# A two-layer hybrid trunk on one core: other buffer counts in the state-space scan, and fewer score maxima ahead of the latent attention

## The chip, the cores and the metric

The kernel runs on one core of one Trainium2 chip. The metric is device time in microseconds from the start to the end of one execution. Besides plain runs there is one execution taken by the hardware profiler. From it come the profile page and the trace that is queried in the text. A core has five engines, each working through its own instructions in order: TensorE (PE; its weight loads are listed as PEld), VectorE (DVE), ScalarE (ACT), GpSimd (POOL) and SyncE (SP). SP does no arithmetic here; it issues almost all DMA transfers. "SPq" and the like name an engine's queue.

## The reference, cut to what matters

Two layers run over 1024 latent tokens and 128 context tokens of width 1024, all in float32. Layer 0 has a window attention and a bidirectional state-space scan beside each other, with one output projection. Layer 1 is a multi-head latent attention with 16 heads. The parts that the change touches:

```python
# layer 0, scan, per chunk of 128 tokens and per head (16 heads, two directions)
decay = jnp.exp(jnp.where(causal, cum_l - cum_s, -inf))
scores = einsum(c, b) * decay
y = scores @ (x * dt) + (c @ h_in) * exp(cum)          # within the chunk + from the state
y = y_f + flip(y_b) + d_skip * xs
s_out = rms_norm(y * silu(z), gnorm_w)                 # gated norm
out = concat([a_out, s_out]) @ w_out                   # projection, then the residual add
...
# layer 1, per head
p = softmax(q @ k.T * scale)                           # latent tokens read 1024 + 128 keys
o = p @ v
```

The softmax needs one number per query that is near the row's maximum, so that the exponentials stay in range. Since the same number is taken off the numerator and the denominator, it need not be the maximum itself.

## The kernel before

**Order of the work.** The kernel is written as Python generators that issue instructions. The tile framework then orders each engine's instructions by a modelled timeline (line 1712), so the order on an engine is not that of the code. Only what goes through `keep_in_program_order` (`pinned`, `in_order`) stays where it was written. Memory is split into four arenas R, S, G and F; `Space.tile` gives a tile `bufs` buffers that take turns. A write to a buffer waits until its last reader is done. There is no other renaming: with `bufs=2` the tile after next shares the buffer.

**The scan, `scan_out` (lines 975 to 1037).** It runs once for each token tile c of 128 tokens: first the context tile (`NLT` = 8), then 0 to 7. It works with features on partitions and tokens along the row. Tiles 8 and 0 are issued beside the gates of layer 0 (`first_outputs`, line 1043). The others are issued in the loop at line 1158, each ahead of the projection (`project_out`) of the tile before.

A tile loads x in both layouts (`xs`, `y`), the gate path z (`zs`), the entering state (`H`) and the small factors B and C. `y`, `xs`, `zs` and `H` are 512 KB each. Then come four units u of four heads each. A unit does this:

- SP loads `cu` (line 1003, 512 KB): the cumulated decays of four heads and two directions, the same row to all 128 partitions.
- ACT takes exponentials for the state part (line 1008, two instructions), and DVE multiplies them by C into `Cx` (1009).
- POOL masks `cu` by direction (1012, two), ACT takes eight biased exponentials (1014), DVE adds the directions (1016) and multiplies by the scores `G` (1017). The result lies in `cu` itself.
- PE multiplies it, and `Cx`, into the accumulator `acc` (line 971, called from 1021).

After units 1 and 3 DVE adds the accumulator to half of `y` (1025) and multiplies that half by `zs` (1026). At the tile's end `split` (ACT copy, line 249; DVE subtraction, line 250) turns `y` into the two halves `sT` of the three-product matmul. ACT then squares `y` into the same `zs` buffer (1029), and DVE sums the squares (1031). `zs` is therefore held until line 1031 is done.

**The projection, `project_out` (line 1091).** It has 72 matmuls of 512 columns per tile, in two accumulators: `acca` for the attention part and `accs` for the scan part, which reads `sT`. Then come `L1105` to `L1108`, the norm of the next layer and its transposes (`L1062` to `L1067`).

**The latent attention's prelude (lines 1586 to 1612).** Heads go in pairs. A pair needs its operands (`AK`, `BK`, `AQ`, `BQ`), the values, and for each head a row of negated maxima in row 96 of `AQ`. `head_max` makes that row: for each token tile, three matmuls of 384 keys (line 1447) and a DVE maximum over each (recorded at line 209, where the step list calls it). The context tile has one of 128 keys. So a head has 8 x 3 + 1 = 25 of them (`NMAX`). After each group of token tiles come the negation (1426, 1427), a transpose on PE (1432), a copy (1437) and one row store per tile (1439). The groups are the tiles 0 to 3, the tiles 4 to 7 and the context tile. Ahead of pair 0 the code issues the values and all 50 maxima of heads 0 and 1.

**The main loop (lines 1614 to 1643).** `pair_main` yields 38 steps per pair: 18 for the queries 0 to 511, 18 for 512 to 1023, two for the context. A step makes one tile of scores (1468 to 1470), the exponential (1475) and, later, the product with the values (1489). `spread` lays other streams beside the steps, at most three units per step: the next pair's operands and the maxima of its two heads, from step 11 on.

Of the kernel before, what the change touches and what calls it, by code (L numbers as in the profile page):

```python
# [12 lines left out]
F32 = mybir.dt.float32  # L13
F32R = mybir.dt.float32r
# [11 lines left out]
NLT = NL // 128  # L26
KT = D // 128
# [193 lines left out]
def hybrid_trunk(ctx: ExitStack, tc: tile.TileContext, I, O, dbg=None, stage=99):  # L221
# [683 lines left out]
    p4, p = Space(mem), Space(mem)  # L905
# [69 lines left out]
    def scan_out(p, sp, c):  # L975
# [13 lines left out]
        y = p.tile([128, KT, 128], F32, tag="y", name="y", bufs=2)  # L989
        dma.dma_start(y, xT_d[:, :, tok].rearrange("k p n -> p k n"))  # L990
        pool.tensor_tensor(y, y, dskip.unsqueeze(2).broadcast_to([128, KT, 128]), ALU.mult)
        zs = p.tile([128, KT, 128], F32, tag="zs", name="zs", bufs=2)
        dma.dma_start(zs, z_d[:, :, tok].rearrange("k p n -> p k n"))
        if c < NLT:
            H = p.tile([128, D], F32, tag="Hc", name="Hc", bufs=2)
            dma.dma_start(H[0:64], H_d[c, 0:64])
            dma.dma_start(H[64:128], H_d[NLT - 1 - c, 64:128])
        for u in range(4):
            g, h0 = u // 2, c * 16 + u * 4
            if u % 2 == 0:  # L1000
                acc = psum("o" if c < NLT else "pre", "yacc")
            cu = p.tile([128, 4, 2, 128], F32, tag="cu", name="cu", bufs=2)
            dma.dma_start(cu, bcast_rows(cum_d[h0:h0 + 4], 128))
            if c < NLT:
                Cx = p.tile([128, 4, 128], F32, tag="Cx", name="Cx", bufs=2)
                for d in range(2):
                    r = slice(d * 64, (d + 1) * 64)
                    act.activation(Cx[r], cu[r, :, d], AF.Exp)  # L1008
                dve.tensor_tensor(Cx, Cx, BC[:, 1, g].unsqueeze(1).broadcast_to([128, 4, 128]), ALU.mult)
            for d in range(2):  # L1010
                s = 1 - 2 * d
                pool.affine_select(cu[:, :, d], cu[:, :, d], [[0, 4], [s, 128]], ALU.is_ge, NEG, base=0, channel_multiplier=-s)  # L1012
                for j in range(4):
                    act.activation(cu[:, j, d], cu[:, j, d], AF.Exp, bias=nb[:, d, h0 + j:h0 + j + 1])  # L1014
            m = cu[:, :, 0]
            dve.tensor_tensor(m, m, cu[:, :, 1], ALU.add)
            dve.tensor_tensor(m, m, G[:, g].unsqueeze(1).broadcast_to([128, 4, 128]), ALU.mult)
            todo = [(xs, m, j) for j in range(4)] + ([(H, Cx, j) for j in range(4)] if c < NLT else [])
            for n, (left, right, j) in enumerate(todo):
                a, b = j % 2, u % 2 * 2 + j // 2  # L1020
                in_order(n, acc[a * 64:(a + 1) * 64, b * 128:(b + 1) * 128], left[:, (u * 4 + j) * 64:(u * 4 + j + 1) * 64], right[:, j],
                         start=(u % 2 == 0 and n < 2), stop=(u % 2 == 1 and n >= len(todo) - 2))
            if u % 2:
                yg, ks = y[:, g * 4:g * 4 + 4], slice(g * 4, g * 4 + 4)
                dve.tensor_tensor(yg, acc.rearrange("p (k n) -> p k n", k=4), yg, ALU.add)
                dve.tensor_tensor(yg, yg, zs[:, ks], ALU.mult)
        sT = sp.tile([128, 2, KT, 128], F32R, tag="sT", name="sT", bufs=2)
        split(sT[:, 0], sT[:, 1], y)
        act.activation(zs, y, AF.Square)
        sq = p.tile([128, 128], F32, tag="sq", name="sq", bufs=1, at="G")  # L1030
        dve.tensor_reduce(sq, zs.rearrange("p k n -> p n k"), AX.X, ALU.add)
# [123 lines left out]
    with p5 as p:  # L1155
        gate = load_gate(p, 0, 1)
        prev = None
        for c in [NLT] + list(range(NLT)) + [None]:
            if c is not None:
                sT = sTs[c] if c in sTs else scan_out(p, op5, c)  # L1160
# [127 lines left out]
    steps = Steps()  # L1288
# [127 lines left out]
            after(1, place, Q, pr, uq_proj(qh, ql, pr * 128, cols), AQ, BQ, cols)  # L1416
            yield

    def head_max(h):

        s = h % NSET

# [15 lines left out]
            for t in range(n):  # L1438
                dma.dma_start(AQ[s][96:97, (t0 + t) * 128:(t0 + t + 1) * 128].bitcast(F32), mrow[t:t + 1].bitcast(F32))

        for t0, n in ((0, 4), (4, 4), (NLT, 1)):
            pm = p7.tile([128, 4, 3], F32, tag="pm", name="pm", bufs=3)
            spans = [(NL + 128, 128)] if t0 == NLT else [(c * CH, CH) for c in range(3)]
            for t in range(t0, t0 + n):
                for c, (k0, w) in enumerate(spans):
                    pp = spare("pp")
                    pe.matmul(pp[:, 0:w], AQ[s][0:96, t * 128:(t + 1) * 128], AK[s][0:96, k0:k0 + w], start=True, stop=True)  # L1447
                    after(1, dve.tensor_reduce, pm[:, t - t0, c:c + 1], pp[:, 0:w], AX.X, ALU.max)
                    if t == t0 + n - 1 and c == len(spans) - 1:
                        after(1, negate, t0, n, pm[:, 0:n, 0:len(spans)])  # L1450
                    yield
# [134 lines left out]
    NMAX = 25  # L1586
# [19 lines left out]
    mem.set("G", F32)  # L1606
    while len(AK) < NSET:
        operand_set()
    rows1 = head_max(1)
    for stream in (first, quad_values(0), head_max(0), rows1):  # L1610
        for _ in stream:
            steps.tick()
    p8, p9 = Space(mem, right=True), Space(mem)
    for pair in range(8):
        op = p7.tile([128, T], F32, tag="op", name="op")
        if pair < 7:
            Q = pair // 2 + 1
            make, n_make = [operands(pair + 1)], 22
            if pair % 2 == 0 and Q < 4:
                make += [quad_weights(Q), quad_rope(Q)]  # L1620
            aux = [(chain(*make), n_make, 0), (chain(head_max(2 * pair + 2), head_max(2 * pair + 3)), 2 * NMAX, 11)]
            if pair % 2:
                aux[0] = (aux[0][0], 22, 0)
                aux.append((quad_values(Q), NKT, 20))
            aux = spread(36, *aux)
            for _ in pair_main(pair, op):
# [89 lines left out]
```

## Time and profile before

| | us |
|---|---|
| median of 3 runs | 1871.18 |
| lowest and highest run | 1867.86 and 1876.07 |
| profiled execution | 1872.8 |
| its span, first to last instruction | 1871.0 |

| engine | busy us | share of the span |
|---|---|---|
| PE | 1696.0 | 91% |
| DVE | 1043.1 | 56% |
| ACT | 865.4 | 46% |
| POOL | 728.0 | 39% |

The shares are averages over stages with different limits. The mean granted clock of PE is 0.946. In the timeline the stages lie about so: modulation and first layer's projections to 350 us, convolutions and window attention to 640, gates and scan and output projection to 1000, the latent projections and gates to 1165, the attention to 1750, the final projection to the end.

### The profile page before, as it was taken

The numbers are of one execution on the slowest core, as the hardware profiler recorded it, in microseconds if no ns is written. First come the engines' busy times: TensorE is split into PE (matmuls) and PEld (weight loads), VectorE is DVE, ScalarE is ACT, GpSimd is POOL, SyncE is SP. The second block draws the span as 40 slices with busy tenths as digits, with TensorE's granted clock in tenths as the row PEclk, the third lists the DMA queues.
The fourth block names the chain that finished last, engine by engine and source line by source line (L and its number), as shares of the span: only waits on it lengthen the run. The fifth ranks groups of instructions, "written<-read, shape, count | busy, mean of one in ns | idle before, by whom it ended". The sixth has DMA issues, their size and how long they took to land.

```text
span 1871.0 us, 26764 instructions
## 1 busy us (share of the span) xinstructions
PE 1696.0 (91%) x8881; PEld 1302.8 (70%) x8881; DVE 1043.1 (56%) x1968; ACT 865.4 (46%) x1932; POOL 728.0 (39%) x728
## 2 busy tenths in 40 slices
PE   6899998998998777879788999999999999999898
PEld 2799997886776665657568899665665665654486
DVE  3755545556555468767656433756665565465243
ACT  4632222556565356566644433345544544545321
POOL 2510000024333335555534010366665574565532
PEclk8999999999999898989889999799998998999999
DMA  6513323345444897766643533011120121113352
GB/s 219 160 54 109 105 66 109 122 123 146 130 133 130 247 276 243 210 187 202 176 144 110 153 116 106 10 56 28 45 72 27 40 61 47 31 33 113 110 157 90
DMA packets 229566, 219.67 MB, mean 117 GB/s; under 512 B 37282, under 2 KB 194544, under 8 KB 229428
## 3 DMA queue, kind: packets, MB, share of 16 engines
q1 hardware_dynamic: 229284, 217.84, 39.3%
q8 instruction: 70, 1.15, 0.3%
q14 instruction: 68, 0.56, 0.1%
q0 software_dynamic: 144, 0.13, 0.0%
HBM read 156.65 MB, written 56.44 MB: 114 GB/s over the span
## 4 chain that ended last, share of the span: by engine, by line
PE 38%; DMA 9%; DVE 5%; ACT 4%; issue 2%; SPq 1%; POOL 1%; DVEq 0%; POOLq 0%; ACTq 0%
PE acco L1489 6%; PE acc L256 5%; PE acc L257 5%; PE acc L258 5%; PE sc L1468 3%; PE pp L1447 3%; PE sc L1470 3%; PE sc L1469 3%; DMA arenaG<-cum_d 2%; DMA arenaF<-rd_d 2%; DMA rd_d<-arenaF 1%; PE den L1520 1%; ACT arenaG L1014 1%; DVE arenaR L250 1%; DVE arenaF L209 1%
## 5 line engine op out<-in xcount | busy, mean ns | idle before, releaser
L1504 POOL TENSOR_TENSOR arenaG<-arenaG 128x512 f32<-128x512 f32 x256 | 334.1, 1324 | 231.0 <-ACT arenaG L1475 199.5
L256 PE MATMUL acc<-arenaR 128*128 128x384 f32 (+4 forms) x1128 | 391.5, 348 | 32.4 <-ACT arenaR L249 11.2
L257 PE MATMUL acc<-arenaR 128*128 128x384 f32 (+3 forms) x1056 | 362.2, 343 | 0.1
L258 PE MATMUL acc<-arenaR 128*128 128x384 f32 (+4 forms) x1032 | 351.1, 341 | 0.1
L1475 ACT ACTIVATE arenaG<-sc 128x512 f32<-128x512 f32 (+1 forms) x304 | 174.8, 580 | 225.2 <-PE sc L1470 217.2
L256 PEld LDWEIGHTS acc<-arenaR 128*128 128x128 f32 x1128 | 218.0, 194 | 67.4 <-ACT arenaR L249 12.9
L209 DVE TENSOR_REDUCE arenaF<-pp 128x1 f32<-128x384 f32 (+1 forms) x400 | 198.8, 540 | 104.2 <-PE pp L1447 102.4
L257 PEld LDWEIGHTS acc<-arenaR 128*128 128x128 f32 x1056 | 203.8, 193 | 12.5 <-issue 2.8
L258 PEld LDWEIGHTS acc<-arenaR 128*128 128x128 f32 x1032 | 199.8, 194 | 12.8 <-DVE arenaR L250 1.6
L250 DVE TENSOR_TENSOR arenaR<-arenaF,arenaR 128x512 fp32r<-128x512 f32 (+2 forms) x144 | 126.8, 892 | 91.9 <-ACT arenaR L249 89.0
L249 ACT CAST arenaR<-arenaF 128x512 fp32r<-128x512 f32 (+3 forms) x160 | 101.1, 647 | 131.1 <-issue 22.4
L1489 PE MATMUL acco<-arenaG 128*64 128x512 f32 (+1 forms) x608 | 152.0, 612 | 0.0
L1447 PE MATMUL pp<-arenaR 96*128 96x384 f32 (+1 forms) x300 | 98.0, 393 | 12.1 <-DVE arenaF L209 11.8
L752 POOL TENSOR_TENSOR arenaG<-arenaS,arenaG 128x512 fp32r<-128x512 f32 x26 | 43.6, 1678 | 157.5 <-PE acco L756 84.0
L1468 PE MATMUL sc<-arenaR 96*128 96x512 f32 (+1 forms) x228 | 95.0, 417 | 4.5 <-ACT arenaG L1475 4.2
L1447 PEld LDWEIGHTS pp<-arenaR 96*128 96x128 f32 x300 | 59.3, 206 | 56.7 <-DVE arenaF L209 28.7
L1014 ACT ACTIVATE arenaG<-arenaG,arenaF 128x128 f32<-128x128 f32 x288 | 88.8, 389 | 14.1 <-POOL arenaG L1012 13.1
L1012 POOL TENSOR_SCALAR_AFFINE_SELECT arenaG<-arenaG 128x512 f32<-128x512 f32 x72 | 60.9, 855 | 83.2 <-ACT arenaF L1008 47.8
L1470 PE MATMUL sc<-arenaR 97*128 97x512 f32 (+1 forms) x228 | 90.9, 402 | 1.2 <-DMA arenaR<-arenaF 1.2
L1469 PE MATMUL sc<-arenaR 96*128 96x512 f32 (+1 forms) x228 | 90.1, 395 | 0.0
L1489 PEld LDWEIGHTS acco<-arenaG 128*64 128x64 f32 x608 | 37.3, 141 | 71.0 <-issue 68.6
L250 DVE TENSOR_TENSOR arenaR<-acc,arenaR 64x512 fp32r<-64x512 f32 (+2 forms) x84 | 48.3, 579 | 62.6 <-ACT arenaR L249 61.2
(333 smaller groups left out, 3444.5 us busy)
## 6 DMA issues: line engine op xcount, KB each, us to landing
arenaF<-in_ada_w_dram SPq DMA_DIRECT2D x96, 256.0 KB
arenaG<-cum_d SPq DMA_DIRECT2D x36, 512.0 KB
arenaF<-in_ab_w_in_dram SPq DMA_DIRECT2D x51, 256.0 KB
z_d<-arenaF SPq DMA_DIRECT2D x24, 192.0 KB
xs_d<-arenaF SPq DMA_DIRECT2D x8, 576.0 KB
arenaF<-xT_d SPq DMA_DIRECT2D x9, 512.0 KB
arenaF<-xs_d SPq DMA_DIRECT2D x9, 512.0 KB
x_d<-arenaG SPq DMA_DIRECT2D x9, 512.0 KB
```

The costliest lines, as they stand in the source:

```text
L209: f()
L250: lo_eng.tensor_tensor(lo, src, hi.bitcast(F32), ALU.subtract)
L256: pe.matmul(out, ah, bh, start=first, stop=False)
L257: pe.matmul(out, ah, bl, start=False, stop=False)
L258: pe.matmul(out, al, bh, start=False, stop=last)
L1447: pe.matmul(pp[:, 0:w], AQ[s][0:96, t * 128:(t + 1) * 128], AK[s][0:96, k0:k0 + w], start=True, stop=True)
L1468: pe.matmul(sc[:, 0:n], AK[s][0:96, ks], BQ[s][:, qs], start=True, stop=False)
L1469: pe.matmul(sc[:, 0:n], BK[s][:, ks], AQ[s][0:96, qs], start=False, stop=False)
L1470: pe.matmul(sc[:, 0:n], AK[s][:, ks], AQ[s][:, qs], start=False, stop=True)
L1475: act.activation(pf, sc[:, 0:n], AF.Exp, scale=SCALE_M)
L1489: put = lambda: pe.matmul(acc[0][a * 64:(a + 1) * 64], V[:, a], pfs[a], start=(i < 2 and k < 2), stop=(last and k >= len(todo) - 2))
L1504: pool.tensor_tensor(totals[a], first[a] if i == 1 else totals[a], pfs[a], ALU.add)
```

## The change

In the scan: `cu` has three buffers and not two, `zs` one and not two. The split of `y` into `sT` is done for each half as soon as that half has been gated. `sT` is taken before the units.

In the prelude: `head_max` takes a list of groups. Only the first group (tiles 0 to 3) of heads 0 and 1 is done ahead of pair 0, 24 maxima, with four of the ten value products laid between them. The other two groups of both heads, 26 maxima, go into pair 0's steps at two per step, ahead of the other streams. In pair 0 the maxima of heads 2 and 3 start at step 13. The removed line that set `aux[0]` again in odd pairs changed nothing.

```diff
-        zs = p.tile([128, KT, 128], F32, tag="zs", name="zs", bufs=2)
+        zs = p.tile([128, KT, 128], F32, tag="zs", name="zs", bufs=1)
...
+        sT = sp.tile([128, 2, KT, 128], F32R, tag="sT", name="sT", bufs=2)
         for u in range(4):
...
-            cu = p.tile([128, 4, 2, 128], F32, tag="cu", name="cu", bufs=2)
+            cu = p.tile([128, 4, 2, 128], F32, tag="cu", name="cu", bufs=3)
...
                 dve.tensor_tensor(yg, yg, zs[:, ks], ALU.mult)
-        sT = sp.tile([128, 2, KT, 128], F32R, tag="sT", name="sT", bufs=2)
-        split(sT[:, 0], sT[:, 1], y)
+                split(sT[:, 0, ks], sT[:, 1, ks], yg)
...
-    def head_max(h):
+    GROUPS = ((0, 4), (4, 4), (NLT, 1))
+
+    def head_max(h, groups=GROUPS):
...
-        for t0, n in ((0, 4), (4, 4), (NLT, 1)):
+        for t0, n in groups:
...
-    rows1 = head_max(1)
-    for stream in (first, quad_values(0), head_max(0), rows1):
-        for _ in stream:
-            steps.tick()
+    for _ in first:
+        steps.tick()
+    values0, rows0 = quad_values(0), chain(*[head_max(h, GROUPS[0:1]) for h in range(2)])
+    for i in range(12):
+        next(rows0)
+        next(rows0)
+        if i % 3 == 2:
+            next(values0)
+        steps.tick()
+    for _ in values0:
+        steps.tick()
+    later0 = chain(*[head_max(h, (g,)) for g in GROUPS[1:] for h in range(2)])
...
-            aux = [(chain(*make), n_make, 0), (chain(head_max(2 * pair + 2), head_max(2 * pair + 3)), 2 * NMAX, 11)]
+            aux = [(chain(*make), n_make, 0), (chain(head_max(2 * pair + 2), head_max(2 * pair + 3)), 2 * NMAX, 11 if pair else 13)]
+            if pair == 0:
+                aux.insert(0, (later0, 72, 0))
             if pair % 2:
-                aux[0] = (aux[0][0], 22, 0)
                 aux.append((quad_values(Q), NKT, 20))
```

## The prediction

> **What bounds the kernel now.** I began with the page's summary, then the table of windows, the chain of work that ended last, the waits, and the timeline of single engines. The change touches two stretches. One is the scan of layer 0 with its output projection: tiles 1 to 7 fill 728 to 970 us. The other is the prelude of the latent attention, 1165 to 1196 us, with pair 0 behind it, 1196 to 1265 us.
>
> ```profile
> 728.00:970.00 242.00, 191.73 (x1094) 147.49 (x1093) 169.00 (x195) 144.73 (x353) 123.50 (x125) 0.87 0.64 192
> 1165.00:1196.00 31.00, 27.92 (x77) 18.01 (x76) 25.07 (x62) 5.14 (x19) 2.54 (x2) 0.60 0.07 17
> 1196.00:1265.00 69.00, 68.21 (x308) 44.05 (x306) 41.58 (x87) 33.00 (x67) 45.51 (x37) 0.98 0.16 44
> ```
>
> The columns are: window, length, then busy time of PE, PEld, DVE, ACT and POOL, granted clock, DMA share, GB/s. In the scan no engine is full. Per tile (242 / 7 = 34.6 us) PE is busy 27.4, at a clock of 0.87, DVE 24.1, ACT 20.7, POOL 17.6. So a chain through several engines sets the pace. In the prelude DVE is busy 25.1 of 31 us and PE runs at a clock of 0.60. Pair 0 is PE's: 68.2 of 69.0.
>
> The chain of work through the scan, and ACT's groups in the same window (count, busy, mean ns, idle before and its releaser):
>
> ```profile
> by line: DMA arenaG<-cum_d 16.4%; ACT arenaG L1014 8.5%; issue 7.8%; PE yacc L971 5.1%; PE accs L256 4.3%; PE acca L256 3.9%; PE accs L257 3.7%; PE accs L258 3.5%; PE acca L257 3.3%; PE acca L258 2.9%; DMA arenaF<-xT_d 2.8%; POOL arenaG L10
> ...
> 904.22 6.83 DMA arenaG<-cum_d
> L1014 ACT ACTIVATE arenaG<-arenaG,arenaF 128x128 f32<-128x128 f32 x224 | 69.0, 389 | 6.6 <-POOL arenaG L1012 5.7
> L1008 ACT ACTIVATE arenaF<-arenaG 64x512 f32<-64x512 f32 x28 | 17.6, 628 | 41.2 <-DMA arenaG<-cum_d 39.0 <-PE yacc L971 1.8
> L1008 ACT ACTIVATE arenaG<-arenaG 64x512 f32<-64x512 f32 x28 | 17.6, 628 | 14.4 <-DMA arenaG<-cum_d 9.2 <-DVE arenaF L1025 2.9 <-PE acca L258 1.9
> ```
>
> The load of the decays, `cu`, is 16.4% of 242 us = 39.7 us of the chain. Seen from ACT it is 39.0 + 9.2 = 48.2 us of idling, 6.9 per tile. With two buffers the load for unit u+2 starts only when the matmuls of unit u have read theirs, and it lasts 6.8 us in the piece quoted.
>
> **The change part by part.**
>
> **Third buffer of `cu`.** No instruction is added; each of the 28 loads of these tiles may start a unit earlier, 34.6 / 4 = 8.6 us now, more than that load lasts. The most that this can give is the 39.7 us. The least is nothing, if the next wait ends at the same moment, and that next wait is visible:
>
> ```profile
> POOL arenaF L991 <- DMA arenaF<-xT_d: 14.5, 4, 6.5
> ```
>
> The wait for `y` (xT_d, 14.5 us on POOL, with `L1012` of the running tile queued behind it) stays. I take half, **-20 us**: 2.9 of 34.6 per tile. That leaves 31.7, still above the busiest engine's 27.4, so no engine forbids it. Ends kept: 0 and -39.7. Tiles NLT and 0 are scanned beside the gates before 728 us; I count them at 0.
>
> **One buffer of `zs`.** This adds a wait: the z load of a tile may start only after the square sum (`L1031`) of the tile just before, where two buffers asked for the one before that. Rows of SP's queue and of DVE:
>
> ```profile
> 762.49 0.44 SPq L1003 DMA_DIRECT2D arenaG<-cum_d  x1
> ...
> 770.09 0.47 SPq L996 DMA_DIRECT2D arenaG<-H_d  x1
> ...
> 776.40 0.72 SPq L993 DMA_DIRECT2D arenaF<-z_d  x1
> 774.36 2.02 DVE L1031 TENSOR_REDUCE arenaG<-arenaF 128x128 f32<-128x1024 f32 x1
> ...
> 792.24 1.75 DVE L1026 TENSOR_TENSOR arenaF<-arenaF,arenaG 128x512 f32<-128x512 f32 x1
> ...
> 807.01 1.96 DVE L1031 TENSOR_REDUCE arenaG<-arenaG 128x128 f32<-128x1024 f32 x1
> ...
> 817.75 0.68 DVE L1026 TENSOR_TENSOR arenaF<-arenaF 128x512 f32<-128x512 f32 x1
> ```
>
> The z load at 776.40 leaves just as tile 1's sum ends (774.36 + 2.02 = 776.38). It is tile 3's, used at 817.75. With one buffer that place belongs to tile 2, which first uses z at 792.24: 15.9 us later. At the next boundary 808.97 to 817.75 leaves 8.8. A load of the same 512 KB takes 6.8 (the `cu` row), so it fits with 2.0 to spare at the narrow one. Behind the waiting issue on SP stand the loads and stores laid after it. They wait only as long as the sum is later than planned, and in the quoted row z left with the sum's end. Cost in the sum: **0**, hidden by units 0 and 1 of the new tile; without that cover it is rival 2.
>
> **Split in halves.** One copy and one subtraction of 1024 columns become two of 512, for 9 tiles. The last halves are shorter and the first half lies at unit 1, where PE may use it.
>
> ```profile
> 737.34 1.05 ACT arenaS L249
> ...
> 933.07 1.05 ACT arenaS L249
> PE accs L256 <- ACT arenaS L249: 18.7, 6, 6.2
> L249 ACT CAST arenaS<-arenaF 128x1024 fp32r<-128x1024 f32 x8 | 8.4, 1044 | 3.6 <-DVE arenaF L1026 3.6
> L249 ACT CAST arenaR<-arenaG 128x512 fp32r<-128x512 f32 x8 | 4.8, 614 | 0.7 <-PE acca L257 0.6
> ```
>
> A copy of 1024 takes 1.04, one of 512 takes 0.61. The copy on the chain becomes 0.43 shorter, and it stands there in five tiles (the first and the last piece are quoted): **-2 us**. ACT pays 2 x 0.61 - 1.04 = 0.18 more per tile, in its idle time. Ends: +1.6 (nine times that 0.18, all on the path) and -18.7 (PE's whole wait for the copy, which the first half could fill with matmuls); I take the chain's figure because PE is not the bound here.
>
> **Fewer maxima before pair 0.** Before, 50 maxima (25 per head) stand ahead of the main loop; after, 24. The others, 26, go into the first steps of pair 0 at two per step, and the maxima of heads 2 and 3 begin at step 13 instead of 11.
>
> ```profile
> L209 DVE TENSOR_REDUCE arenaF<-pp x50: 291/548/559, 1165.6 to 1193.8; 128x1 f32<-128x384 f32 x48, 128x1 f32<-128x128 f32 x2
> 1166.52 5.20 DVE L209 TENSOR_REDUCE arenaF<-pp 128x1 f32<-128x384 f32 x11 [0.33 <-PE pp L1447]
> 1187.41 0.15 DVE L1426 TENSOR_REDUCE arenaF<-arenaF 128x4 f32<-128x12 f32 x1
> ...
> 1192.48 1.19 PE L1470 MATMUL sc<-arenaR 97*128 97x512 f32 x2 [0.52 <-DMA arenaR<-arenaF]
> 1195.44 0.77 PE L256 MATMUL acc<-arenaR 128*128 128x512 f32 x1
> ...
> 1210.41 0.18 PE pp L1447
> L1439 SPq DMA_DIRECT2D arenaR<-arenaF x108: 497/587/1396, 1173.9 to 1680.5; - x108
> ```
>
> DVE makes one in 5.20 / 11 = 0.47 us, so 24 take 11.3; at the mean pace of all 50 (28.2 / 49 = 0.58) they take 13.8. From the last one to the first score that reads its row (negate, transpose, copy, four row stores) pass 1192.48 - 1187.41 = 5.1. The scores of head 1 can then start at 1165.6 + 11.3 to 13.8 + 5.1 = 1182.0 to 1184.5. Now PE works on without such a stop from 1195.4, so 10.9 to 13.4 are saved; I take 12. The 26 moved maxima cost PE, pair 0's bound, 0.18 each = 4.7. The DVE work moved is 26 x 0.47 = 12.2, making 53.8 of 69 us: it fits on the mean, which is why I add nothing for it. With the maxima go ten row stores (two heads, five token tiles), 0.59 each on SP = 5.9 us, in a stretch where the windows row shows a DMA share of 0.16. They are issued by step 13 or soon after, and the scores that read them begin at step 18, so they stay hidden; without those five steps they would cost their 5.1 of latency. The ten value products now stand between the maxima on an idle PE. Net: **-7 us**. Ends: -13 (PE does the moved maxima while it waits for the last row) and +5 (the prelude gains nothing and the 4.7 are paid).
>
> **The sum.** -20 + 0 - 2 - 7 = -29. The profiled execution took 1872.8 (span 1871.0 and 1.8 around it): 1843.8. The median of the runs, 1871.18, lies 1.6 lower; I write **1843 us**. A measurement of this kernel can tell about 0.5% from no change, here 9.4 us.
>
> **A rule beside the row.** A busy POOL holds up DVE here:
>
> ```profile
> 784.30 2.27 DVE L1066 TENSOR_TENSOR arenaF<-arenaF,shift 128x512 f32<-128x512 f32 x1
> ...
> 784.13 1.89 POOL L991 TENSOR_TENSOR arenaF<-arenaF 128x1024 f32<-128x1024 f32 x1
> L1016 DVE TENSOR_TENSOR arenaG<-arenaG 128x512 f32<-128x512 f32 x29 | 26.9, 926 | 19.9 <-ACT arenaG L1014 8.3 <-issue 6.0 <-ACT arenaF L1035 2.8
> L1017 DVE TENSOR_TENSOR arenaG<-arenaG,arenaF 128x512 f32<-128x512 f32 x29 | 25.3, 873 | 0.7
> ```
>
> `L1066` reads two SBUF tensors; it spanned 2.27 us and ended 0.55 after POOL's `L991`, where its neighbour `L1025` (one input in PSUM) averages 0.68 (rows below). `L1016` and `L1017` average 0.93 and 0.87 for the same 512 columns. The Trainium skill, page "SBUF — State Buffer", section "Who interferes with whom", states that a DVE operation with two SBUF inputs and a GpSimd operation that reads SBUF exclude each other for their whole length; the trace agrees with it, and it speaks against packing the scan closer. The sum leaves this out; rival 3 prices it from rows.
>
> ```profile
> L1012 POOL TENSOR_SCALAR_AFFINE_SELECT arenaG<-arenaG 128x512 f32<-128x512 f32 x56 | 48.6, 874 | 57.2 <-ACT arenaF L1008 35.5 <-ACT arenaG L1008 21.2
> ...
> 841.99 1.14 PE yacc L971 x8
> ...
> L1025 DVE TENSOR_TENSOR arenaF<-yacc,arenaF 128x512 f32<-128x512 f32 x15 | 10.2, 683 | 2.9 <-PE yacc L971 2.9
> ```
>
> **The rivals.**
>
> 1. *Forecast*, -29: 1843.8.
> 2. *z is late next.* With the tile 3 us shorter the narrow gap of 8.8 falls towards 6, under the 6.8 of a load, and DVE, in order, stops at `L1026` with all behind it. At 1.7 per tile x 7 = 12 given back: -17, 1856. For it: the 2.0 spare. Against: other boundaries have more (15.9).
> 3. *The port takes the gain.* `L1016` and `L1017` stand (0.93 - 0.68) x 29 + (0.87 - 0.68) x 29 = 12.8 us above 0.68. If units drawn together double that, and the split's 2 is lost too, 15 go: -14. If `L1009` and `L1066` behave alike, some 5 more: -9, **1864**, which counts as no change. This is also where the case belongs that the third buffer does not do what it says, because loads in flight together lengthen each other (DMA share 0.64).
> 4. *Pair 0 becomes DVE's.* If the maxima come in clumps, PE waits for PSUM that DVE has not read, as in the prelude. Then the 7 go: -22, 1851.
> 5. *The whole load goes.* -39.7 - 2 - 10 = -52, 1821. For it: PE's gaps cost double, as a row each side of one stop shows:
>
> ```profile
> 805.22 0.50 PE L256 MATMUL accs<-arenaR,arenaS 128*128 128x512 f32 x1 [2.68 <-ACT arenaS L249]
> ...
> 808.41 0.63 PE L256 MATMUL accs<-arenaR,arenaS 128*128 128x512 f32 x1
> 808.84 0.61 PE L257 MATMUL accs<-arenaR,arenaS 128*128 128x512 f32 x1
> ...
> 809.75 0.40 PE L257 MATMUL accs<-arenaR,arenaS 128*128 128x512 f32 x1
> 809.98 0.40 PE L258 MATMUL accs<-arenaR,arenaS 128*128 128x512 f32 x1
> ```
>
> After an idle 2.68 us the matmuls start 0.43 apart, later 0.23.
>
> 6. *Slower: z holds SP's queue.* If the new tile's first `cu` is laid behind its z, it leaves at 776.40 and not at 762.49. Then a tile is the load 6.8 + unit 0 (two `L1008` 1.3, `L1012` 0.9, eight `L1014` at 0.31, `L1016` 0.9, `L1017` 0.9, the matmuls 1.1: 7.6) + unit 1 at DVE's pace (24.1 / 4 = 6.0) + 16.7 from the first `L1026` to the end of the sum (792.24 to 808.97): 37.1 against 34.6. 2.5 x 7 = +18, with the prelude's -7 a total of +11: **1884**. It decides once a unit's pace is above 5.8 us in that queue order (+9.4). Against it: the order of SP's issues is not that of the code. The code issues z before `H`; the trace issues tile 3's `H` at 770.09 and its z at 776.40.
>
> **How the numbers follow.** Chances: forecast 0.50, z late 0.14, port 0.12, pair 0 0.09, whole load 0.08, slower 0.07. Faster by over 0.5% (below 1861.8) are 1, 2, 4 and 5: 0.81; within it 3: 0.12; slower 0.07. The likeliest case's own range is 1832 to 1856 (a scan of -8 to -32). The range that I give, 1820 to 1866, takes in cases 1 to 5 and leaves out the slower one and the edges.
>
> **What would show it.** Right: the chain through the scan has `cum_d` under 8%, ACT's idle before `L1008` falls below 24 us, and tiles 1 to 7 take about 220 us. z: `L1026` idles for z_d. Port: `L1016` and `L1017` average above 1.1 us. Split: PE's wait for `arenaS L249` falls below 10 us. Prelude: 24 reductions before the first score of head 1, steady matmuls from about 1183 us less what the scan gave, pair 0 about 5 us longer with PE still full; DVE's if PE idles before `L1447` for `L209`. The prediction is wrong if `cum_d` leaves the chain and the scan still takes 235 us or more: then another chain of equal length stood beside it.

## The result, and the profile after

| | before | after |
|---|---|---|
| median, us | 1871.28 (4 runs) | 1848.74 (4 runs) |
| ratio, 95% interval | | 0.9876 (0.9844 to 0.9908) |
| span of the profiled execution | 1871.0 | 1849.4 |
| last store of the second gates (latent attention begins) | 1163.8 | 1148.5 |
| first store of an attention output, pair 0 | 1259.6 | 1240.5 |
| last store of an attention output | 1782.0 | 1760.0 |

So 22.5 us were gained by the medians, and 21.6 between the two profiled spans: 15.3 up to the end of the second gates, 6.7 from there to the last store of an attention output, and 0.4 lost behind that. In the changed kernel the lines of the scan lie one further on (the exponentials of the state part are `L1009`, the mask `L1013`, the gating `L1027`), those of the attention two further on (`L1449`, `L1472`); `L1031`, `L1105` and `L1111` keep their numbers.

First the scan. These are the table of windows for 728 us to the end of tile 7, the chain of work through it, and the waits in it (engine, line, releaser: us in total, times, longest), of the changed kernel:

```profile
728.00:957.00 229.00, 192.67 (x1117) 149.08 (x1116) 170.58 (x197) 138.92 (x342) 119.92 (x120) 0.91 0.65 197
```
```profile
by line: DMA arenaG<-cum_d 9.0%; DMA arenaF<-xT_d 8.2%; ACT arenaG L1015 7.6%; issue 7.5%; PE accs L256 7.3%; PE accs L257 6.3%; PE accs L258 6.1%; PE yacc L971 6.0%; PE acca L256 4.7%; PE acca L257 4.1%; PE acca L258 4.1%; DMA h_d<-arenaF 
```
```profile
PE Gp L984 <- ACT arenaF L1105: 26.2, 4, 13.2
POOL arenaF L991 <- DMA arenaF<-xT_d: 20.7, 5, 5.9
...
ACT arenaG L1009 <- DMA arenaG<-cum_d: 18.1, 5, 7.3
...
DVE arenaF L1027 <- DMA arenaF<-z_d: 5.8, 2, 4.0
```

The load of the decays fell from 39.7 us of the chain to 9.0% of 229 = 20.6, and ACT's wait for it from 48.2 to 18.1. The load of `y` took its place in part: 8.2% = 18.8 us of the chain against 2.8% of 242 = 6.8 before. PE's 18.7 us of waiting for the copy `L249` are gone from the list; its wait of 26.2 us at `L984` for `L1105` was 3.7 before.

The end of a tile is the end of `L1031`. The rows of tile 0 and tile 2, of the changed kernel:

```profile
714.86 2.03 DVE L1031 TENSOR_REDUCE arenaG<-arenaF 128x128 f32<-128x1024 f32 x1
...
804.59 1.93 DVE L1031 TENSOR_REDUCE arenaG<-arenaF 128x128 f32<-128x1024 f32 x1
```

In the same way for every kernel that was run (start plus duration, us; the last column is the time from tile 2's end to tile 7's end, divided by 5):

| kernel | tile 0 ends | tile 2 ends | tile 7 ends | per tile, 3 to 7 |
|---|---|---|---|---|
| before | 744.8 | 809.0 | 970.6 | 32.3 |
| changed | 716.9 | 806.5 | 956.4 | 30.0 |
| e1_prelude | 751.0 | 815.9 | 973.8 | 31.6 |
| e1_scan | 718.0 | 806.0 | 953.2 | 29.4 |
| e1_cu3 | 724.9 | 808.9 | 941.4 | 26.5 |
| e1_split | 744.1 | 809.2 | 980.8 | 34.3 |
| e2_cu3_prelude | 720.7 | 804.3 | 936.9 | 26.5 |
| e2_zs1 | 744.4 | 816.9 | 979.4 | 32.5 |
| e2_xstore | 716.6 | 803.5 | 957.4 | 30.8 |
| e2_cu3_late | 747.5 | 810.3 | 952.3 | 28.4 |
| e3_after | 719.3 | 809.8 | 957.3 | 29.5 |
| e3_cu3_prelude | 723.2 | 810.2 | 944.8 | 26.9 |
| e3_halves_end | 718.2 | 806.1 | 953.5 | 29.5 |
| e3_yact | 726.3 | 802.5 | 950.4 | 29.6 |

Two things are to be seen. In the changed kernel tile 0 ends 27.9 us earlier than before, and by tile 2 only 2.5 of that is left. And the steady tiles gain 2.3 us each, not the 2.9 that the forecast had for all seven. The forecast's base was off as well: it divided the window from 728 us by seven and got 34.6 a tile, but tile 0 ends only at 744.8, and from tile end to tile end a tile of before takes 32.3.

Now the attention. PE (with one earlier row to compare) and then DVE at the end of pair 0 and in pair 1, timeline of the changed kernel (start, duration, engine, line; in brackets the idle time before and who ended it):

```profile
1171.30 1.94 PE L1491 MATMUL acco<-arenaG 128*64 128x512 f32 x8
...
1240.50 2.99 PE L1449 MATMUL pp<-arenaR,arenaS 96*128 96x384 f32 x6 [0.17 <-ACT arenaF L1439]
...
1244.46 1.22 PE L1472 MATMUL sc<-arenaS,arenaR 97*128 97x512 f32 x2 [0.25 <-DMA arenaS<-arenaF]
...
1273.25 0.69 PE L1449 MATMUL pp<-arenaR 96*128 96x384 f32 x1 [2.81 <-DVE arenaF L209]
1273.73 0.63 PE L1470 MATMUL sc<-arenaR 96*128 96x512 f32 x1
1274.16 0.63 PE L1471 MATMUL sc<-arenaR 96*128 96x512 f32 x1
...
1276.74 3.08 PE L1491 MATMUL acco<-arenaG 128*64 128x512 f32 x8
```
```profile
1240.35 4.46 DVE L209 TENSOR_REDUCE arenaF<-pp 128x1 f32<-128x384 f32 x10
...
1270.77 1.95 DVE L1292 TENSOR_TENSOR arenaF<-arenaF 128x128 f32<-128x128 f32 x2 [2.34 <-DMA arenaF<-rd_d]
```

DVE is late at the end of pair 0: ten reductions in a row take 4.46 us, and PE's six products beside them take 2.99, 0.50 each. In pair 1 PE stands 2.81 us for a reduction, and the scores behind it start 0.43 us apart; eight value products behind them take 3.08 us, which took 1.94 at 1171.30. This second stop is no clump of reductions: DVE itself had stood 2.34 us for a load (`rd_d`) before `L1292`, and the reduction that PE waits for comes behind `L1292` in its order. The windows show both stops: from the end of the second gates to the first store of an output, and the 50 us behind that, of the changed kernel and then of before:

```profile
1148.50:1240.50 92.00, 86.87 (x387) 56.20 (x385) 59.43 (x135) 40.54 (x95) 48.16 (x39) 0.98 0.14 39
1240.50:1290.50 50.00, 46.66 (x182) 26.78 (x182) 27.59 (x57) 22.79 (x46) 24.56 (x19) 0.86 0.11 32
```
```profile
1163.80:1259.60 95.80, 92.72 (x371) 60.14 (x370) 61.51 (x139) 37.49 (x85) 46.78 (x38) 0.86 0.13 35
1259.60:1309.60 50.00, 48.06 (x222) 29.59 (x222) 31.27 (x68) 26.73 (x58) 28.52 (x22) 1.00 0.14 38
```

The low clock of the prelude (0.86 before, 0.98 now) has moved into the 50 us behind it (1.00 before, 0.86 now), and in those 50 us PE got through 182 recorded matmuls where it had 222. How the lead came and went can be counted on the rows of the exponentials (`L1475` before, `L1477` now), one by one, from the end of the second gates. The changed kernel is 14 us ahead at the 25th, 11 at the 40th, 5 at the 41st (behind the ten reductions), still 5 at the 53rd, and 0.6 behind at the 57th (after the stop in pair 1).

### The profile page after: what moved, and what is told of

Read it like the earlier page. It is cut to its first block, busy times and chain, and to the rows that moved or that the text cites. A ratio compares the mean times of both kernels' runs of the same rounds, so it can differ in the third digit from the quotient of the medians.

```text
span 1849.4 us, 26784 instructions
## 1 busy us (share of the span) xinstructions
PE 1679.6 (91%) x8881; PEld 1293.5 (70%) x8881; DVE 1047.0 (57%) x1977; ACT 866.1 (47%) x1941; POOL 731.0 (40%) x728
## 4 chain that ended last, share of the span: by engine, by line
PE 65%; DMA 13%; ACT 5%; DVE 5%; issue 3%; POOL 2%; SPq 2%; POOLq 0%; DVEq 0%; ACTq 0%
PE acc L256 11%; PE acc L258 10%; PE acc L257 10%; PE acco L1491 6%; PE pp L1449 3%; PE sc L1470 3%; PE sc L1472 3%; PE sc L1471 3%; DMA arenaG<-cum_d 2%; DMA arenaF<-rd_d 2%; DMA rd_d<-arenaF 2%; ACT arenaG L1015 2%; DMA arenaF<-xT_d 1%; PE st L811 1%; DVE arenaR L250 1%
## 5 line engine op out<-in xcount | busy, mean ns | idle before, releaser
L1477 ACT ACTIVATE arenaG<-sc 128x512 f32<-128x512 f32 (+1 forms) x304 | 174.7, 580 | 219.1 <-PE sc L1472 210.8
L209 DVE TENSOR_REDUCE arenaF<-pp 128x1 f32<-128x384 f32 (+1 forms) x400 | 199.2, 539 | 110.2 <-PE pp L1449 108.7
L257 PEld LDWEIGHTS acc<-arenaR 128*128 128x128 f32 x1056 | 203.9, 193 | 12.6 <-issue 2.8
L249 ACT CAST arenaR<-arenaF 128x512 fp32r<-128x512 f32 (+3 forms) x160 | 101.0, 648 | 135.0 <-DMA arenaF<-in_ab_w_in_dram 24.2
L1015 ACT ACTIVATE arenaG<-arenaG,arenaF 128x128 f32<-128x128 f32 x288 | 89.8, 390 | 26.6 <-POOL arenaG L1013 26.1
L1449 PE MATMUL pp<-arenaR 96*128 96x384 f32 (+1 forms) x300 | 91.9, 362 | 11.0 <-DVE arenaF L209 10.5
L1449 PEld LDWEIGHTS pp<-arenaR 96*128 96x128 f32 x300 | 54.7, 190 | 54.2 <-DVE arenaF L209 23.5
L1472 PE MATMUL sc<-arenaR 97*128 97x512 f32 (+1 forms) x228 | 89.0, 394 | 1.3 <-DMA arenaR<-arenaF 1.3
L573 POOL TENSOR_TENSOR arenaF<-arenaF 128x256 f32<-128x256 f32 (+1 forms) x27 | 18.4, 684 | 160.1 <-DVE arenaF L571 94.6
L1013 POOL TENSOR_SCALAR_AFFINE_SELECT arenaG<-arenaG 128x512 f32<-128x512 f32 x72 | 61.7, 869 | 50.0 <-ACT arenaF L1009 28.1
```

What stands on the lines that cost most here:

```text
L209: f()
L257: pe.matmul(out, ah, bl, start=False, stop=False)
L1472: pe.matmul(sc[:, 0:n], AK[s][:, ks], AQ[s][:, qs], start=False, stop=True)
L1477: act.activation(pf, sc[:, 0:n], AF.Exp, scale=SCALE_M)
```

## The experiments

The planner lays every kernel out anew, so an edit also changes orders in places that it does not touch. The runs were therefore read by their time and by the table of tile ends together. All ratios are against the kernel before on the same chip; the e1 runs share one chip, the e2 runs another and the e3 runs a third. One kernel was timed on two of them (e2_cu3_prelude and e3_cu3_prelude) and came out at 0.9885 and 0.9837, half a per cent or 9 us apart. A difference of that size between runs of different chips is therefore weak evidence.

### Each part alone

**e1_prelude** and **e1_scan** divide the diff at `head_max`: everything from `GROUPS` on, or everything ahead of it.

> Only the latent attention's prelude is changed (24 maxima ahead of pair 0, the other 26 in pair 0, heads 2 and 3 from step 13); the scan is that of before. Theory A (the two traces of before and after: the first maximum to the last store of o moved by -22.0 +15.3 = -6.7 us behind the gates): 6 to 8 us less than before, ratio 0.9957 to 0.9968, and nothing else moves. Rival B (the planner laid the whole program out anew, so that the prelude's part and the scan's part do not add): less than 3 us either way here, and the scan alone then carries 20 or more.

> Only the scan is changed (three buffers of cu, one of zs, the output split in two halves); the prelude is that of before. Theory A: 15 us less than before (the last store of the gates' second part moved from 1163.8 to 1148.5), ratio 0.992. The prediction on record had 22 for this part (ratio 0.988). Rival B (the parts do not add): 20 or more here, with the prelude alone under 3.

Measured: e1_prelude 1874.48 us against 1874.94, ratio 1.0 (0.9979 to 1.0022). e1_scan 1861.33, ratio 0.9922 (0.9892 to 0.9952). The scan alone came out as theory A had it. The prelude alone is worth nothing that can be seen, so A was wrong there; but the scan does not carry 20 either, so B in its form is not supported. What the profile of e1_prelude shows is the shift named above: from the end of the second gates to the first store 90.2 us instead of 95.8, and behind that

```profile
1258.70:1308.70 50.00, 46.67 (x181) 27.04 (x181) 27.38 (x58) 23.02 (x47) 23.76 (x19) 0.84 0.12 32
```

with the same stop of 2.82 us for `L209` in pair 1. That stop is not the new prelude's alone. All eight profiles with the new prelude have it (2.81 to 3.09 us), but so do two of the six with the old one, e1_cu3 and e1_split; in the other four it is 1.08 to 1.10 us. In e1_cu3:

```profile
1267.18 0.44 PE L1447 MATMUL pp<-arenaR 96*128 96x384 f32 x1 [2.81 <-DVE arenaF L209]
```

The low clock right behind the first store, at the end of pair 0, does go with the new prelude: over those 10 us the clock is 0.50 to 0.66 in the eight, 1.00 in five of the six and 0.83 in the sixth (e2_cu3_late). Over all profiles of this study the stretch up to the first store takes 95.4 to 96.9 us in the six with the old prelude, and 90.2 to 92.7 in the eight with the new one (means 96.0 and 91.6). From the first store to the last the old ones take 523.0 on average (520.8 to 524.9), the new ones 526.3 (519.5 to 531.7). So 4.4 are gained and about 3.3 given back. The 6.7 of the changed kernel's first profile do not repeat: its second one, e3_after, takes 91.2 + 527.0 = 618.2 us over the two stretches, and before takes 95.8 + 522.4 = 618.2.

The parts do not add up to the whole: 0.9922 and 1.0 alone, 0.9876 together, some 8 us more. The intervals overlap, and the profiled spans do not show these 8 us (1851.3 for e1_scan, 1849.4 and 1855.8 for the changed kernel), so where they come from stays open.

**e1_cu3, e1_split, e2_zs1** divide the scan's part; each has the old prelude. e1_cu3 (with the one buffer of `zs` that makes the room):

```diff
-        zs = p.tile(..., tag="zs", name="zs", bufs=2)
+        zs = p.tile(..., tag="zs", name="zs", bufs=1)
...
-            cu = p.tile(..., tag="cu", name="cu", bufs=2)
+            cu = p.tile(..., tag="cu", name="cu", bufs=3)
```

e2_zs1 has the first of these two edits alone, e1_split only the split inside the loop.

> Scan with three buffers of cu and one of zs, but one split of 1024 columns at the tile's end, as before; old prelude. Theory A (the third buffer carries the scan's gain, the split in halves is worth 2 us): 12 to 14 us less than before, ratio 0.9925 to 0.9936, and PE waits for the copy L249 into arenaS by about the 18.7 us of before. Rival C (the halves are what gave it, because PE's wait for the copy went from 18.7 us to under 2): 5 us less at most, ratio above 0.997.

> Only the split in halves; two buffers of cu, two of zs, old prelude. Theory A: 0 to 3 us less than before, ratio 0.9984 to 1.0; cum_d stays at about 16% of the chain through the scan. Rival C (the halves gave the scan's gain): 10 us less or more, ratio below 0.9947, with PE's wait for the copy into arenaS gone from its 18.7 us.

> Before with one buffer of zs alone: two buffers of cu, one split at the end, old prelude. Theory (the prediction's: the load of z is hidden by units 0 and 1 of its tile): ratio 0.998 to 1.002. Rival Z (z is late: L1026 stands for z_d, 1.7 us in each of 7 tiles): 12 us more, ratio 1.006, and a line of L1026 waiting for z_d of about 12 us.

Measured: e1_cu3 1852.13 us, ratio 0.987 (0.9847 to 0.9892). e1_split 1891.73, ratio 1.0085 (1.0057 to 1.0114). e2_zs1 1878.68, ratio 1.0044 (1.0026 to 1.0063).

The third buffer gives all of the scan's gain and more: e1_cu3 lies 9.2 us under e1_scan on one chip, though it lacks the split. Rival C is out. Theory A was off in two ways: it had 12 to 14 us, and it had PE's wait for the copy into arenaS unchanged at about 18.7. That wait is gone from the list of e1_cu3 (728 to 942 us) without any split in halves. The split alone costs 16 us, while it does what it was counted for: PE's wait for the copy into arenaS, 12.5 us in this stretch before, is 6.1.

```profile
ACT arenaF L1009 <- DMA arenaG<-cum_d: 25.5, 10, 4.8
ACT arenaG L1009 <- DMA arenaG<-cum_d: 18.8, 7, 6.2
...
PE accs L256 <- ACT arenaS L249: 6.1, 5, 2.2
```

These are waits of e1_split from 744 to 980 us. ACT still stands 25.5 + 18.8 = 44.3 us for the decays, and their load is 22.6% of the chain here: the wait that was shortened was not the one that set the pace. Why the tiles became slower (34.3 us) is not shown by this run.

In e2_zs1 no wait of `L1026` for z_d shows, so rival Z was wrong in its place, and the theory's nothing was wrong in size. The loss is one stop, at tile 1: it takes 39.3 us (783.7 - 744.4) where before took 31.6 (the profiled execution is the longest of twelve). SP's queue in e2_zs1 (start, issue time, line, transfer):

```profile
744.69 0.39 SPq L993 DMA_DIRECT2D arenaF<-z_d  x1
...
750.30 0.35 SPq L1095 DMA_DIRECT2D arenaG<-in_x_sample_dram  x1
...
754.68 0.36 SPq L1067 DMA_DIRECT2D h_d<-arenaF  x1
755.14 0.94 SPq L1003 DMA_DIRECT2D arenaG<-cum_d  x2
```

Two loads of decays stand behind other loads and behind a store (`L1067`) whose data are not there before 754.6. Before, the same two left at 745.32 and 752.04. Like the forecast's slower rival this is a matter of the order in SP's queue, at one boundary and for 7.7 us; but z is not what holds it, since z left at 744.84 before and at 744.69 here.

By ratios, 0.987 against 1.0044, the third buffer by itself would be worth 1.7%, some 32 us, of which the single buffer of `zs` takes 8. That is an estimate: it supposes that the two add, the two were timed on different chips, and no run has three buffers of `cu` beside two of `zs`.

### Why the split costs

**e2_cu3_prelude** and **e3_cu3_prelude** are one kernel: the changed one with the split put back to one piece of 1024 columns at the tile's end. **e3_after** is the changed kernel, beside it on one chip. **e3_halves_end** is e3_cu3_prelude with

```diff
-        split(sT[:, 0], sT[:, 1], y)
+        for ks in (slice(0, 4), slice(4, 8)):
+            split(sT[:, 0, ks], sT[:, 1, ks], y[:, ks])
```

> The changed kernel without the split in halves: three buffers of cu, one of zs, one split of 1024 columns at the tile's end, new prelude. Theory S (the split in halves costs about 9 us, because in the runs with it the issue queue SP stands before stores whose data are not ready, with the next tile's loads behind them: 28 us of the 229 in the changed kernel, none in e1_cu3): 1.3% of the scan part from e1_cu3, and 0.2 to 0.4% of the prelude on top, ratio 0.983 to 0.985, tiles 3 to 7 about 27 us apart. Rival P (the prelude is worth nothing, as in e1_prelude): ratio 0.987, and the time from the first part of the gates' end to the end is that of e1_cu3 within 2 us. Rival N (the halves cost nothing; e1_scan and e1_cu3 differ by the planner's luck): ratio 0.988 to 0.992, as the changed kernel.

> The changed kernel once more, beside e3_cu3_prelude on one chip, since it was timed in four executions only and e1_scan (0.9922) and e2_xstore (0.9948), which end the gates' second part at the same place in their profiles (1145.6 and 1147.8 against 1148.5), came out slower. Theory S (the split in halves costs 8 to 10 us of the scan): ratio 0.990 to 0.993, above e3_cu3_prelude by 0.003 or more. Rival N (the halves cost nothing in the whole): ratio 0.986 to 0.989, within 0.002 of e3_cu3_prelude.

> e2_cu3_prelude once more, for the comparison with e3_after on one chip. Theory S: ratio 0.984 to 0.9885, tiles 3 to 7 about 27 us apart. Rival N: the same ratio as e3_after within 0.002.

> e2_cu3_prelude with the one split of 1024 columns at the tile's end replaced by two of 512 at the same place, one right behind the other: the first half is not earlier, and ACT pays 0.18 us more per tile. The planner then lays SP's queue out as in the changed kernel (a stretch of the store of x, xs, H, x, y, z) and not as in e2_cu3_prelude (y, z, cu, the store of x). Theory O (that order is what costs): tiles 3 to 7 are 29 to 31 us apart instead of 27, POOL's L991 stands for xT_d by about 20 us, ratio 0.003 to 0.006 above e3_cu3_prelude. Rival E (what costs is the first half among the scan's own work on ACT and DVE): tiles 27 apart as in e2_cu3_prelude and the same ratio within 0.002.

Measured: e2_cu3_prelude 1848.05 us, ratio 0.9885 (0.9858 to 0.9911). On one chip: e3_cu3_prelude 1847.16, ratio 0.9837 (0.9815 to 0.986); e3_after 1854.92, 0.9876 (0.9849 to 0.9903); e3_halves_end 1860.82, 0.9908 (0.9885 to 0.9932). The first of these ratios fitted rivals P and N, not theory S; against the changed kernel's 0.9876, which was not timed beside it, it shows no cost of the halves at all. The second comparison fits S in its difference, 7.8 us, though e3_after lies lower than S had it and its interval touches the other's.

The windows of tiles 3 to 7 show where the time is, in this order: before, e3_after, e3_halves_end, e3_cu3_prelude.

```profile
808.97:970.60 161.63, 128.24 (x745) 99.14 (x744) 107.80 (x131) 95.31 (x236) 78.67 (x81) 0.88 0.60 177
```
```profile
809.80:957.30 147.50, 127.62 (x759) 99.17 (x760) 119.56 (x137) 93.78 (x235) 82.73 (x83) 0.92 0.68 198
```
```profile
806.10:953.50 147.40, 128.50 (x760) 100.46 (x761) 120.63 (x139) 95.36 (x236) 79.96 (x83) 0.92 0.65 198
```
```profile
810.20:944.80 134.60, 122.79 (x746) 96.01 (x743) 117.09 (x128) 94.27 (x229) 82.55 (x84) 0.95 0.71 209
```

With one split PE is busy 122.8 of 134.6 us, 24.6 of 26.9 a tile at a clock of 0.95; there PE is nearly the bound. With two (e3_halves_end) it idles 19 us instead of 12, and its busy time grows by 5.7: 14 more recorded matmuls in the window are some 2.3 of it, the rest goes with the lower clock. No engine's busy time accounts for 13 us. e3_halves_end has the same data flow as e3_cu3_prelude, with the first half not a moment earlier, and goes at the pace of the changed kernel (29.5 a tile). Theory O holds in the pace and rival E falls: what costs is not that the first half lies among the scan's work. Theory O's wait was smaller than it had it, 11.9 us for `y` at `L991` and not 20, and the ratio rose by 0.007, more than its 0.003 to 0.006. What did change is the order that the planner laid. SP's queue over one tile of e3_cu3_prelude, and then of e3_halves_end (where the store of x is `L1112`):

```profile
864.41 0.37 SPq L990 DMA_DIRECT2D arenaF<-xT_d  x1
866.31 0.38 SPq L993 DMA_DIRECT2D arenaF<-z_d  x1
866.79 0.52 SPq L1003 DMA_DIRECT2D arenaG<-cum_d  x1
867.41 0.38 SPq L1111 DMA_DIRECT2D x_d<-arenaG  x1
```
```profile
849.41 0.58 SPq L981 DMA_DIRECT2D arenaF<-bc_d  x1
858.34 0.33 SPq L1112 DMA_DIRECT2D x_d<-arenaG  x1
859.41 0.33 SPq L1003 DMA_DIRECT2D arenaG<-cum_d  x1
859.78 0.45 SPq L988 DMA_DIRECT2D arenaF<-xs_d  x1
860.33 0.47 SPq L996 DMA_DIRECT2D arenaG<-H_d  x1
860.84 1.50 SPq L997 DMA_DIRECT2D arenaG<-H_d  x1
862.51 0.47 SPq L1003 DMA_DIRECT2D arenaG<-cum_d  x1
863.08 0.37 SPq L1096 DMA_DIRECT2D arenaG<-in_x_sample_dram  x1
864.49 0.37 SPq L990 DMA_DIRECT2D arenaF<-xT_d  x1
866.54 0.45 SPq L993 DMA_DIRECT2D arenaF<-z_d  x1
```

In the first the loads of `y`, z and the decays leave within 2.4 us of each other at the tile's end, and the store of x behind them. In the second SP issues nothing from 849.99 to 858.34, in front of the store of x; then eight loads, 3.5 MB in all, leave within 7.1 us.

**e2_xstore** and **e3_yact** move one member of that clump off SP, in the changed kernel:

```diff
-        dma.dma_start(x1_d[tok], x)
+        act.dma_start(x1_d[tok], x)
```
```diff
-        dma.dma_start(y, xT_d[:, :, tok].rearrange("k p n -> p k n"))
+        act.dma_start(y, xT_d[:, :, tok].rearrange("k p n -> p k n"))
```

> The changed kernel, with only the store of x (L1111) issued from ACT's queue in place of SP's, so that loads behind it on SP no longer wait for POOL's L1108. Theory S (SP's queue is held by stores): tiles 3 to 7 fall from 29.9 to 27 to 28 us apart, 8 to 13 us less than the changed kernel, ratio 0.981 to 0.984. Rival N (the halves cost by themselves, on ACT and DVE): tiles stay 29 to 30 apart, ratio 0.986 to 0.990. Rival H (the other stores on SP, L1067 of h_d, hold the queue in its place): SP stands before L1067 for 25 us or more, ratio as rival N.

> The changed kernel with the load of y (xT_d, L990) issued from ACT's queue instead of SP's. ACT has just squared the tile whose buffer the load takes, so it has nothing to wait for, and the load no longer stands on SP behind a cu that waits for its buffer. Theory O: POOL's wait at L991 falls from 21 us to under 8, tiles 3 to 7 fall from 29.5 to 28 us apart or less, 5 to 10 us less than e3_after. Rival Q (the other loads of the clump, cu and z behind them, are as late as y): L991 no longer waits, yet tiles stay 29 to 30 apart and the ratio is that of e3_after within 0.002.

Measured: e2_xstore 1860.97 us, ratio 0.9948 (0.9929 to 0.9968), 30.8 us per tile. e3_yact 1854.59, 0.9881 (0.9858 to 0.9905), 29.6 per tile. POOL's wait for `y` over tiles 3 to 7, in e3_after, in e2_xstore, in e3_yact and, to compare, in e3_cu3_prelude:

```profile
POOL arenaF L991 <- DMA arenaF<-xT_d: 17.4, 4, 5.0
```
```profile
POOL arenaF L991 <- DMA arenaF<-xT_d: 21.0, 4, 7.4
```
```profile
POOL arenaF L991 <- DMA arenaF<-xT_d: 13.6, 4, 8.4
```
```profile
POOL arenaF L991 <- DMA arenaF<-xT_d: 1.0, 2, 0.6
```

Moving either one alone did not give the pace back. Without the store in SP's queue theory S's 8 to 13 us did not come; e2_xstore was slower than every forecast for it, and slower than the changed kernel (0.9876, not timed beside it). With `y` out of SP's queue the wait went from 17.4 to 13.6 and the tiles stayed 29.6 apart, which is rival Q in time but not in its wait. The kernel with one split waits 1.0 us there, and 1.9 for the decays (e3_after: 15.5), so the loads do come late in the orders with two. So it is shown that two pieces in place of one, at the same place, cost some 2.6 us per tile, where ACT's extra work is 0.18. That the order laid around them is the cause is argued from the rows and not tested by itself. Which of its waits costs is not shown either; POOL's, ACT's and PE's orders differ between the two as well, and these runs do not separate them from SP's.

### Where the early lead goes

**e2_cu3_late** is e1_cu3 in which the third buffer is set aside at the first tile's first unit and put back after tile 0's last:

```diff
+            ring = p.rings["cu"][0]
+            if c == NLT and u == 0:
+                third.append(ring.pop())
+            elif c == 0 and u == 3:
+                ring.append(third.pop())
```

> e1_cu3 with the third buffer of cu in use only from tile 1 on; tiles 8 and 0, scanned beside the gates, have two. Theory G (the 20 us that tile 0 ends earlier in e1_cu3 is lost again by tile 2, since the projection waits for the out weights and gates, whose loads then end later): tile 0 ends at about 744 as before, tiles 2 to 7 still 27 us apart, total within 4 us of e1_cu3, ratio 0.985 to 0.989. Rival L (the early lead is carried to the end): 10 to 20 us more than e1_cu3, ratio 0.993 to 0.998.

Measured: 1859.72 us, ratio 0.9937 (0.9916 to 0.9958). By its time this is rival L, by its tile ends it is theory G. Without the early lead tile 0 ends at 747.5, 22.6 later than in e1_cu3, and tile 2 at 810.3, 1.4 later. That part of theory G holds: the lead is gone by tile 2. What is lost against e1_cu3, 12 us by the ratios of two chips and 10.9 at tile 7's end, is lost behind it, where the order came out otherwise (tiles 28.4 apart on average, the longest 33.9). The last instructions of the gates' product (`L956`) and of the out weights (`L253`), in the view by line of before and then of the changed kernel (after the count: shortest, median and longest in ns; first and last start in us), say what the lead was paid with:

```profile
L956 POOL TENSOR_TENSOR arenaG<-arenaG x12: 995/1014/1630, 627.5 to 724.4; 128x384 f32<-128x384 f32 x12
L253 DVE SCALAR_TENSOR_TENSOR arenaR<-arenaF,vecs,arenaR x9: 739/743/1489, 660.2 to 726.7; 128x512 fp32r<-128x512 f32 x9
```
```profile
L956 POOL TENSOR_TENSOR arenaG<-arenaG x12: 992/1017/1475, 626.6 to 731.3; 128x384 f32<-128x384 f32 x12
L253 DVE SCALAR_TENSOR_TENSOR arenaR<-arenaF,vecs,arenaR x9: 734/750/1115, 664.9 to 734.9; 128x512 fp32r<-128x512 f32 x9
```

The gates and the out weights, which the projection needs, begin their last piece 6.9 and 8.2 us later. The scan's loads went ahead of theirs: by 690 us eight loads of decays had left SP where five had, and the last load of the out weights left at 731.5 where it had left at 720.8.

## Why the prediction was right, and where it was not

The forecast was 1843 in a range of 1820 to 1866; 1848.7 was measured, and faster was right. By its terms:

- **Third buffer, -20.** Right in kind and undersized. With the single `zs` that it needs it measured -24 (e1_cu3), and by the estimate above about -32 by itself, within the ends 0 and -39.7 and nearer the far one. The step that failed is the half: with one split the tiles run at 26.5 to 26.9 us, close to PE's 24.6, not at the 31.7 counted with. (From the true base of 32.3 a gain of 2.9 would have been 29.4.) The clock rose with it (0.88 to 0.95 over tiles 3 to 7), which the forecast had only in rival 5.
- **Tiles 8 and 0, counted at 0.** They gained 27.9 us and kept 2.5 by tile 2. Nothing in the end, but not for nothing: their loads went ahead of those of the gates and the out weights.
- **One `zs`, 0.** Measured +8. The gaps of 8.8 and 15.9 us were read at later boundaries and do hold; it is tile 1 that stops, and not at `L1026` (5.8 us there, as `L1027`, in the changed kernel) but at loads of decays behind other loads and a store.
- **Split, -2.** The sign was wrong: +16 alone, and about +8 on top of the third buffer (9.2 and 7.8 us, each pair on one chip). The end of +1.6 was far too near, since it counted ACT's own 0.18 us per tile and not that the planner's order could change with an edit that moves nothing.
- **Prelude, -7.** The profile fitted (-6.7), but by chance: the second profile of the same kernel gives 0. The saving itself was forecast well. Steady matmuls began 31.6 us behind the gates' end before and 19.0 now, 12.6 saved where 12 were counted. The step that failed is "it fits on the mean, which is why I add nothing". At the end of pair 0 the lead falls by 6 us at the clump of reductions, which is rival 4. Another 5 go at the stop in pair 1, which no rival had: there DVE is late because it waited for a load, and two kernels with the old prelude have that stop too. Alone the prelude is worth 0 within 0.2%.

So the total came near partly by luck: the third buffer's surplus covered what the split and `zs` lost, and the prelude gave nothing that can be seen alone. These terms come to about -32 + 8 + 8 = -16 us, as e1_scan does (-15), and the rest of the 22.5 is the open difference between the parts and the whole. Of the signs named: ACT's idle before the exponentials was to fall below 24 us and is 26.1 + 2.7 = 28.8, of which 18.1 is for the decays; `cum_d` under 8% of the chain narrowly did not come (9.0%); tiles 1 to 7 were to take about 220 us and take 229, read from 728 us as in the forecast. PE's wait for the copy fell below 10 us, but this sign says nothing of the split, since e1_cu3 has it without. The port's rival has two parts. `L1009`, which it named in the second place, did rise, from 0.84 and 0.88 us to 1.00 and 0.97 (now `L1010`), 3.4 us over its 26 operations. Its own sign did not come: the two DVE operations, here `L1017` and `L1018`, average 0.87 and 0.91 us and not above 1.1:

```profile
L1018 DVE TENSOR_TENSOR arenaG<-arenaG,arenaF 128x512 f32<-128x512 f32 x26 | 23.7, 914 | 0.7 <-ACT arenaF L986 0.2
L1017 DVE TENSOR_TENSOR arenaG<-arenaG 128x512 f32<-128x512 f32 x26 | 22.7, 874 | 12.1 <-POOL arenaG L1108 4.4 <-issue 3.3 <-ACT arenaG L1015 3.3
```

The kernel without the split in halves (e3_cu3_prelude) is the fastest that was run: 7.8 us under the changed one at the medians on one chip, with intervals that just overlap. On another chip the same kernel had 0.9885, so its lead over the changed one is likely but not settled.

## What to carry to other kernels

Where a planner lays out the order, time each part of a change alone: two parts of this one took back a good part of what the third had gained, and the profile of the whole looked as if all three had worked. A wait that shrinks in the list (PE's for the copy) is worth nothing while another engine's wait sets the pace, and it may go for another reason than the edit that was meant for it. And work moved off a slow stage must be counted against the busiest stretch that it lands in, not against the mean of the stage.

## What the runs showed of the hardware

In the scan of before a PE stop of 2.68 us was followed by matmuls 0.43 us apart; in pair 1 of the changed kernel one of 2.81 us was. The stop that stands at about the same place in before is shorter,

```profile
1285.26 0.44 PE L1447 MATMUL pp<-arenaR 96*128 96x384 f32 x1 [1.08 <-DVE arenaF L209]
```

and there the granted clock over 1259.6 to 1309.6 stayed at 1.00. The length of a single stop does not decide it, though. At the end of pair 0 of the changed kernel the longest is no longer than that,

```profile
1238.73 0.45 PE L1449 MATMUL pp<-arenaR,arenaS 96*128 96x384 f32 x1 [1.07 <-DVE arenaF L209]
```

but several short ones of 0.17 to 0.36 us follow it, and over 1240.5 to 1250.5 the clock was 0.66. In e1_cu3 the matmuls behind the stop of 2.81 us were still 0.23 apart for 1.6 us and slowed down only then (eight value products in 3.39 us).

What the low clock cost behind the stop in pair 1 of the changed kernel can be estimated from its rows: (1276.74 - 1273.25) / 2 = 1.7 us at half pace and 3.08 - 1.94 = 1.1 us in the eight products, 2.8 in all, about as much again as the stop itself.
